# Sums of squares on VectorE alone, and another order of the paired units in a decoder layer

## The chip, the cores and the metric

The kernel runs on one core of a Trainium2 chip. The metric is the time of one execution in microseconds on the device (us), the median of several runs. The engines are called as in the profile: PE (TensorE, matmuls), PEld (its weight loads), DVE (VectorE), ACT (ScalarE), POOL (GpSimd) and SP (SyncE, whose queue issues the loads).

## The reference, cut to what matters

One decoder layer in fp32 on x of 1024 tokens by 1024 channels. The change touches the two feed-forward blocks and the gate columns of the projection in between, and the norms ahead of them:

```python
def rmsnorm(x, g):
    y = x * lax.rsqrt(jnp.mean(x * x, axis=-1, keepdims=True) + EPS)
    return y * g
def swiglu(x, w_gu, w_down):
    g, u = jnp.split(x @ w_gu, 2, axis=-1)
    return (jax.nn.silu(g) * u) @ w_down

x = x + 0.5 * swiglu(rmsnorm(x, ffn1_norm), ffn1_w_gu, ffn1_w_down)
h = rmsnorm(x, mix_norm);  z = h @ w_in
gates = jax.nn.sigmoid(z[..., COL_GATE:] + b_gate)
merged = gates_A * (y_a @ w_a) + gates_B * (y_b @ w_b) + gates_C * (y_c @ w_c)
x = x + merged @ w_out
x = x + 0.5 * swiglu(rmsnorm(x, ffn2_norm), ffn2_w_gu, ffn2_w_down)
```

## The kernel before

**Layout and precision.** The channels lie on the partitions, the tokens on the free axis, in two halves of 512. An x4 or w4 tile holds two rows of 128 channels by 512 tokens (128x1024). A matmul in fp32 is made of three in the type fp32r (`mm3`, L144 to L146): each operand is split into a high part, a cast on ACT (L132), and a low part, a subtraction on DVE (L133); the three products are high by high, high by low and low by high. `split_later` issues the cast and returns the subtraction as a function to be called later.

**Units.** `Seven` multiplies two by two blocks with seven products in place of eight. A unit f is one such block multiplication; its four blocks of weights are a11, a12, a22, a21, and four sums of them (s1 to s4) are made on DVE by `sums`. `weights` splits them in four parts: "a" (a11, a12), "s" (s2, s1), "t" (s3, s4), "l" (a22). The moving operands are the blocks of the normed x (b11, b12, b21, b22) and their sums t1 to t4, made and split by `OpNorm`. A product is four times three matmuls over the channels. Products go to banks of PSUM; partial sums are kept in SBUF rows: p1 is ACT's copy of a11 by b11, v1 is p1 plus s2 by t2. a12 by b21 is accumulated into the bank that p1 is copied from. `emit(f, i, half, ...)` finishes one quarter of the result: in `SwiGLU` a silu on ACT, additions and the gating multiplication on DVE, in `Gates` a sigmoid on ACT.

**Paired units.** Where the norm of the second half of the tokens is not ready, two units go together: `Seven.units`. It starts with the two products of each unit that need half 0 alone (s3, s4). Between their 16 pieces (counted by n) it places the sums over the channels of half 1 (`norm.tokens`, small matmuls of 128x1), the reciprocal root on DVE (`norm.root`) and the turn of the result into a row (`norm.turn`, PE transposes into a bank). Then follow a11, a12, s2, s1, and last a22 by t4. This happens at three places: units 1 and 2 of the first feed-forward block (the opening, from `SwiGLU.start`), units 0 and 1 of the gates, and units 0 and 1 of the second feed-forward block (ffn2). Behind each pair a single `unit` follows (3, 2 and 2). The functions in `asides` are called one by one at fixed places of `units`: the fetch of the next unit's weights and `ready`, which prepares its "a" part and its sums.

**Opening.** Unit 0 of the first block is multiplied in plain fp32 (`rows`: two matmuls a row of channels) while x arrives: `feed` squares a row on ACT and scales it with the gain; then sums of squares, root and turn follow for that half. The products are scaled by the norm afterwards: `leave` copies the banks, `keep` the scale, `finish` multiplies and does silu and gating.

**Sums of squares.** `square` issues a row's square and returns the addition into the half's accumulator (DVE). With `plain` no addition is made: the square is kept and the token sum, which is a matmul with a column of ones, takes one matmul more per 128 tokens for each such row.

**What sets the order.** In these three stretches the order on PE, DVE, ACT (and SP in the first two) is as the code is written, and each engine works through its instructions in that order.

Of the kernel before, what the change touches and what calls it, by code (L numbers as in the profile page):

```python
# [16 lines left out]
P = 128  # L17
# [25 lines left out]
class Kernel:  # L43
# [322 lines left out]

    def token_sums(self, accs, late=False, bank=None):


        n = accs[0].shape[-1] // P  # L370
        b = (bank or self.bank)()[:, :n]
        for t in range(n):
            for m, acc in enumerate(accs):
                i = self.nc.tensor.matmul(
                    b[:, t:t + 1], acc[:, t * P:(t + 1) * P], self.ones, start=m == 0, stop=m == len(accs) - 1)
                if late and t == 0 and m == 0:
                    self.after(i, self.last)
        return b
# [47 lines left out]
    def latent(self, h):  # L426
# [10 lines left out]
        def c_q(hf):  # L437
            acc, cols = None, slice(hf * 512, hf * 512 + 512)
            for j, d in enumerate(cq):
                b = self.bank()  # L440
                for k in range(DT):
                    self.mm3(b, w[j * DT + k], h[hf][k], k == 0, k == DT - 1)
                acc = self.norm_feed(acc, b, 512)
                self.split_gain(d[0][:, cols], d[1][:, cols], b, self.g_cq[:, j:j + 1])
            nc.vector.tensor_scalar(
                eps[:, hf * 4:hf * 4 + 4], self.token_sums([acc]), EPS / QR, EPS * EPS, op0=ALU.mult, op1=ALU.add)

# [223 lines left out]
    def mem_kv(self, p, filler):  # L671
# [4 lines left out]
        with tc.tile_pool(name="memkv", bufs=1) as q:  # L676
# [11 lines left out]
            fill(2)  # L688
            r = self.rms(self.token_sums([acc], late=True), ML // P, D)
            fill(2)  # L690
# [286 lines left out]
    def project(self, merged, norm, sink):  # L977

        nc, a = self.nc, self.a
        tasks = []  # L980
        for half in range(2):
            for c in range(DT):
                w = self.load(a["w_out"][c])
                b = self.bank()
                for k in range(DT):
                    self.mm3(b, w[k], merged[half][k], k == 0, k == DT - 1)
                x = norm.x(half, c)
                nc.vector.tensor_tensor(x, x, b, op=ALU.add)
                norm.feed(half, c, half == 1 and c == DT - 1)
# [17 lines left out]
    def run(self):  # L1007
# [12 lines left out]
        with tc.tile_pool(name="f1", bufs=1) as fp, self.banks("f1ps") as self.pm:  # L1020
# [15 lines left out]
            def sink(half, c):  # L1036
                add = norm.square(half, c, half == 1 and c >= DT - 2)
                keep(x1d, rows, half, c)
                return add
# [13 lines left out]
            with tc.manual_schedule(engines={E.PE, E.SP, E.DVE, E.Activation}):  # L1053
# [6 lines left out]
                     (6, 4): [do(gates.turned, 0), do(gates.sums, 1)]},  # L1060
                    late)
                gates.units(
                    (0, 1), {0: gates.w0[0], 1: {}}, ([(1, "t")], [(0, "a")]),
                    [lambda: None, do(gates.fetch, 2, [self.x4, gates.w4]), do(gates.ready, 2, [self.x4, gates.w4])])
                gates.unit(2, True)
# [4 lines left out]
        with tc.tile_pool(name="f2", bufs=1) as fp, self.banks("f2ps") as self.pm:  # L1070
# [9 lines left out]
            E = mybir.EngineType  # L1080
            with tc.manual_schedule(engines={E.PE, E.DVE, E.Activation}):
                ffn.units(
                    (0, 1), (), ([(0, "a"), (1, "a")], [(0, "s")]),
                    [lambda: None, lambda: ffn.fetch(2, [self.x4] * 2), lambda: ffn.ready(2)])
                ffn.spill(0, ffn.w4)
                ffn.unit(2, True)
# [22 lines left out]
class OpNorm:  # L1109
# [7 lines left out]
    def __init__(self, k, rows, gain, scaled=False):  # L1117
        self.k, self.x, self.t, self.gain, self.scaled = k, rows, rows, gain, scaled
        self.acc, self.r, self.s, self.op, self.rows, self.plain = {}, {}, {}, {}, {}, {}

    def feed(self, half, c, plain=False):
        self.square(half, c, plain)()

    def square(self, half, c, plain=False):

# [9 lines left out]

        if plain:
            self.plain.setdefault(half, []).append(sq)
            return lambda: None
        return add

    def tokens(self, half):
        k = self.k
        self.s[half] = k.token_sums(
            [self.acc.pop(half), *self.plain.pop(half, ())], late=k.last is not None)

# [73 lines left out]
class Seven:  # L1219
# [66 lines left out]
    def unit(self, f, after=False):  # L1286
# [3 lines left out]
        if not w:  # L1290
            self.sums(f)
            w |= self.weights(f, "a")
        w |= self.weights(f, "s")
        a, x, y = (k.single(), k.single(), k.bank()) if after else (k.bank(), k.single(), k.single())
# [23 lines left out]
    def ready(self, f, rooms=None):  # L1318

        self.made[f] = self.weights(f, "a")  # L1320
        self.sums(f, rooms)

    def units(self, fs, w=(), fill=((), ()), asides=()):
# [22 lines left out]
        for n, (u, (out, s, t), j) in enumerate(  # L1346
                (u, p, j) for u in fs for p in ((y[u], "s3", "t3"), (x[u], "s4", "b22")) for j in range(4)):
            self.product(out, w[u], s, t, js=(j,))
            if n == 1 and not known:
                norm.tokens(1)  # L1350
# [3 lines left out]
                for p in fill[1]:  # L1354
                    more(*p)
            if n == 4 and not known:
                norm.turn(1)
# [115 lines left out]
class SwiGLU(Seven):  # L1473
# [41 lines left out]
    def start(self, load_x, load_g):  # L1515
# [7 lines left out]

        def feed(half, c, plain=False):
            add = norm.square(half, c, plain)
            x, g = norm.x(half, c), norm.gain()[:, c:c + 1]
            if half == 0:
                v.tensor_scalar(x, x, g, None, op0=ALU.mult)
                add()
            else:  # L1530
# [39 lines left out]
        with k.tc.manual_schedule(engines={E.PE, E.DVE, E.Activation, E.SP}):  # L1570
# [29 lines left out]
            b22()  # L1600
            for c in (4, 5):
                feed(1, c, True)
            norm.high(1)
            norm.put("t3", 0, t3)
            leave(0)
            norm.low(1)
            for c in (6, 7):
                feed(1, c, True)
# [10 lines left out]
            leave(1)  # L1619
            self.units(  # L1620
                (1, 2), w, (),
                [lambda: keep(1), lambda: self.fetch(3, [k.x4] * 2), lambda: self.ready(3)])
            finish()
# [268 lines left out]
```

## Time and profile before

| | |
|---|---|
| runs | 2229.87, 2232.82, 2233.83 us; median 2232.82 |
| profiled execution | 2229.82 us, span 2228.1 us, mean granted PE clock 0.995 |
| busy: PE, DVE, ACT, POOL | 2199.7, 1542.7, 894.5, 259.3 us |
| paired units start: opening, gates, ffn2 | 47.3, about 670, about 1585 us |
| the unit behind the pair starts its second-last products | 102.40, 723.69, 1641.65 us |

Rows of the profile name engine, line, operation, tiles as out<-in, sizes and count. Times in a timeline are from the start of the span. A busy PE is one with a matmul under way; its granted clock is a share of the full clock. An fp32 matmul leaves two records, one in fp32r leaves one.

### The profile page before, as it was taken

The page shows a single profiled execution, that of the slowest core. Times are in us where ns is not written, and L with a number is a line of the kernel's source. Part 1 is how long each engine was busy: PE and PEld are TensorE (multiplying, and loading weights), DVE is VectorE, ACT ScalarE, POOL GpSimd, SP SyncE. Part 2 cuts the span into 40 slices and gives each one's busy share as a digit, 9 for nine tenths or more (in the row PEclk, how much of TensorE's full clock was granted, in tenths as well). Part 3 has the DMA queues.
Part 4 walks back from the last instruction along what each step waited for, and adds up shares of the span by engine and source line. Part 5 has one row for each costly group of instructions (what it writes and reads, how often), then busy time and mean ns, then how long its engine had stood idle before and what let it go on. Part 6 is the DMA issues. An engine that isn't in the chain of part 4 may idle for free.

```text
span 2228.1 us, 27721 instructions
## 1 busy us (share of the span) xinstructions
PE 2199.7 (99%) x10376; PEld 1834.7 (82%) x10376; DVE 1542.7 (69%) x2397; ACT 894.5 (40%) x1498; POOL 259.3 (12%) x252
## 2 busy tenths in 40 slices
PE   9899999999999999999999999999989999999999
PEld 5688888888887888888888889988878888888887
DVE  6866666679888655457575769885876666657784
ACT  5422222243455433344244559843432222224432
POOL 0121212100000000013000131140012121210000
PEclk9999999999999999999999999999999999999999
DMA  4233332285332333225161550084033333328543
GB/s 143 79 125 99 110 103 95 88 330 191 121 116 95 115 116 128 92 79 181 39 213 49 201 196 29 30 318 174 29 99 114 99 114 100 114 93 302 181 128 104
DMA packets 113062, 285.92 MB, mean 128 GB/s; under 512 B 13344, under 2 KB 21664, under 8 KB 112800
## 3 DMA queue, kind: packets, MB, share of 16 engines
q1 hardware_dynamic: 112928, 284.16, 37.1%
q8 instruction: 81, 1.33, 0.2%
q14 instruction: 53, 0.43, 0.1%
HBM read 201.80 MB, written 82.31 MB: 128 GB/s over the span
## 4 chain that ended last, share of the span: by engine, by line
PE 92%; DVE 5%; ACT 1%; issue 1%; DMA 0%; DVEq 0%; ACTq 0%
PE one L146 13%; PE bank L144 13%; PE one L144 13%; PE bank L146 13%; PE bank L145 13%; PE one L145 13%; PE mm L144 3%; PE mm L145 3%; PE mm L146 3%; PE bank L881 1%; PE bank L419 1%; PE bank L896 1%; DVE wlo L133 1%; PE bank L897 1%; PE one L1539 1%
## 5 line engine op out<-in xcount | busy, mean ns | idle before, releaser
L132 ACT CAST whi<-x 128x1024 fp32r<-128x1024 f32 (+1 forms) x189 | 178.8, 951 | 454.2 <-PE one L145 198.0
L1284 DVE TENSOR_TENSOR t<-t,one 128x512 f32<-128x512 f32 x178 | 122.2, 686 | 242.0 <-PE one L146 242.0
L144 PE MATMUL bank<-h,whi 128*128 128x512 f32 x644 | 250.8, 390 | 0.0
L145 PE MATMUL bank<-h,whi 128*128 128x512 f32 x644 | 250.7, 389 | 0.0
L146 PE MATMUL bank<-h,wlo 128*128 128x512 f32 x644 | 250.5, 389 | 0.0
L133 DVE TENSOR_TENSOR wlo<-x,whi 128x1024 fp32r<-128x1024 f32 (+1 forms) x189 | 226.7, 1204 | 33.5 <-ACT whi L132 33.5
L144 PE MATMUL one<-h,whi 128*128 128x512 f32 x476 | 186.1, 391 | 0.0
L146 PE MATMUL one<-h,wlo 128*128 128x512 f32 x476 | 185.3, 389 | 0.0
L145 PE MATMUL one<-h,whi 128*128 128x512 f32 x476 | 185.2, 389 | 0.0
L146 PE MATMUL one<-w,wlo 128*128 128x512 f32 x392 | 154.4, 394 | 5.6 <-DVE wlo L133 5.6
L144 PE MATMUL one<-w,whi 128*128 128x512 f32 x392 | 154.5, 394 | 5.5 <-ACT whi L132 5.5
L145 PE MATMUL one<-w,whi 128*128 128x512 f32 x392 | 154.1, 393 | 0.0
L127 ACT CAST whi<-w 128x1024 fp32r<-128x1024 f32 (+1 forms) x108 | 95.1, 899 | 143.7 <-PE one L145 55.2
L128 DVE TENSOR_TENSOR wlo<-w,whi 128x1024 fp32r<-128x1024 f32 (+1 forms) x108 | 110.1, 1033 | 60.6 <-ACT whi L127 60.5
L146 PEld LDWEIGHTS bank<-h,wlo 128*128 128x128 f32 x644 | 120.9, 188 | 25.2
L145 PEld LDWEIGHTS bank<-h,whi 128*128 128x128 f32 x644 | 120.9, 188 | 24.8
L144 PEld LDWEIGHTS bank<-h,whi 128*128 128x128 f32 x644 | 120.9, 188 | 24.8
L145 PE MATMUL bank<-wlo,whi 128*128 128x512 f32 x352 | 136.9, 389 | 0.0
L144 PE MATMUL bank<-whi 128*128 128x512 f32 x352 | 136.9, 389 | 0.0
L146 PE MATMUL bank<-whi,wlo 128*128 128x512 f32 x352 | 136.9, 389 | 0.0
L1636 POOL TENSOR_TENSOR raw<-raw 128x512 f32<-128x512 f32 x39 | 64.1, 1645 | 593.4 <-DVE raw L1494 593.4
L128 DVE TENSOR_TENSOR wlo<-h,whi 128x512 fp32r<-128x512 f32 x130 | 88.1, 713 | 26.5 <-ACT whi L127 26.5
(385 smaller groups left out, 5070.4 us busy)
## 6 DMA issues: line engine op xcount, KB each, us to landing
x<-in_ffn_w_gu_dram SPq DMA_DIRECT2D x78, 512.0 KB, 5.1
w<-tdt SPq DMA_DIRECT2D x40, 512.0 KB, 4.3
tdb<-raw SPq DMA_DIRECT2D x64, 256.0 KB, 2.1
h<-in_ffn_w_down_dram SPq DMA_DIRECT2D x64, 256.0 KB, 6.0
w<-tdb SPq DMA_DIRECT2D x30, 512.0 KB, 4.6
tdt<-w SPq DMA_DIRECT2D x48, 256.0 KB, 2.0
gate<-raw SPq DMA_DIRECT2D x23, 512.0 KB, 2.6
tdt<-raw SPq DMA_DIRECT2D x40, 256.0 KB, 3.1
```

The costliest lines, as they stand in the source:

```text
L127: self.nc.scalar.copy(hi, src)
L128: return (eng or self.nc.vector).tensor_tensor(lo, src, hi.bitcast(F32), op=ALU.subtract)
L132: self.nc.scalar.copy(hi, src)
L133: return lambda: self.nc.vector.tensor_tensor(lo, src, hi.bitcast(F32), op=ALU.subtract)
L144: mmul(out, s[0], m[0], start=first, stop=False, **kw)
L145: mmul(out, s[0], m[1], start=False, stop=False, **kw)
L146: self.last = mmul(out, s[1], m[0], start=False, stop=last, **kw)
L419: nc.tensor.transpose(b[:m, k * P:(k + 1) * P], s, self.ident)
L881: nc.tensor.transpose(b[:, at:at + P], prs[t][:, kk * P:(kk + 1) * P], self.ident)
L896: nc.tensor.matmul(o, w, pt[0], start=n == 0, stop=False)
L1284: return self.nc.vector.tensor_tensor(out, x, y, op=ALU.add)
L1636: sub = lambda d, x, y: nc.gpsimd.tensor_tensor(d, x, y, op=ALU.subtract)
```

## The change

Five edits:

- `plain` is gone: every square is added on DVE, and a token sum is four matmuls. There are 36 fewer small matmuls, and two more additions in half 0 of the opening, four in half 1, two in the gates and one in ffn2.
- In `units` the token sums stand behind piece 3 (were behind 1), the turn behind 6 (was 4). The cast and split of unit f's "s" weights goes ahead of the other unit's copy p1. At the end, the split of a unit's a22 and half of t4, the sum p1 and that unit's `emit` stand together, unit by unit; before, both units' splits came ahead of both sums.
- `ready` is now a generator in three steps. The cast of the next unit's "a" weights is issued ahead of the pair's first silu or sigmoid; its split, the sums, and the cast and split of "s" go ahead of the last additions, the gating, and in the opening `finish`. Before, "s" was cast and split in the next `unit`.
- The opening: sums and turn of half 0 stand behind rows 0 to 3 and row 4; additions go behind splits; in half 1 all of the norm stands behind row 5, and the turn behind row 7.
- In ffn2 other parts of the weights stand around the root (`fill`).

The diff, cut:

```diff
@@ token_sums @@
-        for t in range(n):
-            for m, acc in enumerate(accs):
-                i = self.nc.tensor.matmul(
-                    b[:, t:t + 1], acc[:, t * P:(t + 1) * P], self.ones, start=m == 0, stop=m == len(accs) - 1)
+        for t in range(n):
+            i = self.nc.tensor.matmul(
+                b[:, t:t + 1], acc[:, t * P:(t + 1) * P], self.ones, start=True, stop=True)
@@ gates and ffn2, the calls @@
+                third = gates.ready(2, [self.x4, gates.w4])
                 gates.units(
                     (0, 1), {0: gates.w0[0], 1: {}}, ([(1, "t")], [(0, "a")]),
-                    [lambda: None, do(gates.fetch, 2, [self.x4, gates.w4]), do(gates.ready, 2, [self.x4, gates.w4])])
+                    [lambda: None, do(gates.fetch, 2, [self.x4, gates.w4]), do(next, third), do(next, third)])
...
                 ffn.units(
-                    (0, 1), (), ([(0, "a"), (1, "a")], [(0, "s")]),
-                    [lambda: None, lambda: ffn.fetch(2, [self.x4] * 2), lambda: ffn.ready(2)])
+                    (0, 1), (), ([(0, "a")], [(1, "a")]),
+                    [lambda: None, lambda: ffn.fetch(2, [self.x4] * 2), lambda: next(third), lambda: next(third)])
@@ Seven.ready @@
-        self.made[f] = self.weights(f, "a")
+        self.made[f], low = self.weights_later(f, "a")
+        yield
+        low()
         self.sums(f, rooms)
+        self.made[f] |= self.weights(f, "s")
+        yield
@@ Seven.units @@
-            if n == 1 and not known:
+            if n == 3 and not known:
                 norm.tokens(1)
...
-            if n == 4 and not known:
+            if n == 6 and not known:
                 norm.turn(1)
...
             nc.scalar.copy(p1[u], a[u])
-        more(f, "s")
+            if u == f:
+                more(f, "s")
...
             d, low[u] = self.weights_later(u, "l")
             w[u] = {**w[u], **d}
+        aside()
         for u in fs:
             self.emit(u, 0, 1, None, a[u])
...
             low[u]()
             t4[p]()
-        for u in fs:
             self.mark = self.add(p1[u], p1[u], z[u])
             self.emit(u, 1, 0, p1[u], y[u])
@@ SwiGLU.start @@
-                feed(0, c, c >= 6)
+                feed(0, c)
             rows(0, range(4))
             norm.sums(0)
-            rows(0, (4, 5))
+            rows(0, (4,))
             norm.turn(0)
-            rows(0, (6, 7))
+            rows(0, (5, 6, 7))
...
-            rows(1, range(5))
-            norm.tokens(1)
+            rows(1, range(6))
+            norm.sums(1)
+            rows(1, (6, 7))
+            norm.turn(1)
             self.sums(2)
-            norm.root(1)
-            rows(1, (5, 6))
-            norm.turn(1)
-            rows(1, (7,))
             w[2] = self.weights(2, "t")
             leave(1)
```

**Half 1 of the opening on PE.** The rows named L1539 before and L1546 now are the plain matmuls of unit 0 (x_140 to x_146 are two rows of channels of half 1 each); 128x1 are token sums, 128x128 the turn, L144 the first piece of the pair. Before:

```order
L1539 MATMUL one<-x_144,w_122 128x512
L1539 MATMUL one<-x_144,w_123 128x512
L374 MATMUL bank<-ones,t 128x1 x20
L1539 MATMUL one<-x_144,w_122 128x512
L1539 MATMUL one<-x_144,w_123 128x512
L1539 MATMUL one<-x_146,w_122 128x512
L1539 MATMUL one<-x_146,w_123 128x512
L386 MATMUL bank<-ident,rs_y 128x128 x4
L1539 MATMUL one<-x_146,w_122 128x512
L1539 MATMUL one<-x_146,w_123 128x512
L144 MATMUL one<-h_268,whi 128x512
```

And now:

```order
L1546 MATMUL one<-x_144,w_122 128x512
L1546 MATMUL one<-x_144,w_123 128x512
L1546 MATMUL one<-x_144,w_122 128x512
L1546 MATMUL one<-x_144,w_123 128x512
L373 MATMUL bank<-ones,t 128x1 x4
L1546 MATMUL one<-x_146,w_122 128x512
L1546 MATMUL one<-x_146,w_123 128x512
L1546 MATMUL one<-x_146,w_122 128x512
L1546 MATMUL one<-x_146,w_123 128x512
L385 MATMUL bank<-ident,rs_y 128x128 x4
L144 MATMUL one<-h_262,whi 128x512
```

The sums moved behind one more row and are four instead of 20; the turn moved behind the last row.

**The end of the pair on DVE, in the opening.** L133 are splits: `wlo` of 128x512 a unit's a22, x4 of 128x1024 half of t4, `wlo` of 128x1024 the next unit's weights. L1284 (now L1281) are additions. Before:

```order
L133 TENSOR_TENSOR wlo_529<-w4_135,whi_528 128x512
L133 TENSOR_TENSOR x4_580<-x4_144,x4_579 128x1024
L133 TENSOR_TENSOR wlo_532<-w4_149,whi_531 128x512
L133 TENSOR_TENSOR x4_598<-x4_146,x4_597 128x1024
L1284 TENSOR_TENSOR t_470<-t_470,bank_538 128x512
L1284 TENSOR_TENSOR raw_534<-t_470,one_362 128x512
L1284 TENSOR_TENSOR t_472<-t_472,bank_551 128x512
L1284 TENSOR_TENSOR raw_536<-t_472,bank_364 128x512
L133 TENSOR_TENSOR wlo_633<-x4_486,whi_632 128x1024
```

And now:

```order
L133 TENSOR_TENSOR wlo_511<-w4_135,whi_510 128x512
L133 TENSOR_TENSOR x4_565<-x4_144,x4_564 128x1024
L1281 TENSOR_TENSOR t_452<-t_452,bank_523 128x512
L1281 TENSOR_TENSOR raw_519<-t_452,one_344 128x512
L133 TENSOR_TENSOR wlo_514<-w4_149,whi_513 128x512
L133 TENSOR_TENSOR x4_583<-x4_146,x4_582 128x1024
L1281 TENSOR_TENSOR t_458<-t_458,bank_536 128x512
L1281 TENSOR_TENSOR raw_521<-t_458,bank_346 128x512
L133 TENSOR_TENSOR wlo_517<-x4_468,whi_516 128x1024
```

The first unit's two additions moved ahead of the second unit's splits.

**The end of the pair and the start of unit 3 on ACT, in the opening.** L132 are casts (x4_564 and x4_582 now are t4; `whi` from x4_468, x4_618 and x4_619 are unit 3's "a", "s" and "t" weights), L1498 (now L1501) the pair's silus, L1565 (now L1572) those of `finish`, and the copy is p1 of unit 3. Before:

```order
L1498 ACTIVATE raw_534<-one_442 128x512
L1498 ACTIVATE raw_536<-one_455 128x512
L132 CAST x4_579<-x4_144 128x1024
L132 CAST x4_597<-x4_146 128x1024
L132 CAST whi_632<-x4_486 128x1024
L1498 ACTIVATE t_470<-t_470 128x512
L1498 ACTIVATE t_472<-t_472 128x512
L1565 ACTIVATE t_272<-t_272 128x512
L1565 ACTIVATE t_358<-t_358 128x512
L132 CAST whi_677<-x4_636 128x1024
L1297 COPY t_696<-one_681 128x512
```

And now:

```order
L132 CAST whi_516<-x4_468 128x1024
L1501 ACTIVATE raw_519<-one_424 128x512
L1501 ACTIVATE raw_521<-one_437 128x512
L132 CAST x4_564<-x4_144 128x1024
L132 CAST x4_582<-x4_146 128x1024
L132 CAST whi_624<-x4_618 128x1024
L1501 ACTIVATE t_452<-t_452 128x512
L1501 ACTIVATE t_458<-t_458 128x512
L1572 ACTIVATE t_268<-t_268 128x512
L1572 ACTIVATE t_340<-t_340 128x512
L1295 COPY t_678<-one_663 128x512
```

Unit 3's first cast moved ahead of the pair's first silus, its second from behind `finish` to ahead of the last four silus; the copy stays behind them.

More of the change, by code (lines that the diff above doesn't have):

```diff
@@ L365, in norm_feed, with token_sums @@
         return acc
-    def token_sums(self, accs, late=False, bank=None):
-        n = accs[0].shape[-1] // P
+    def token_sums(self, acc, late=False, bank=None):
+        n = acc.shape[-1] // P
         b = (bank or self.bank)()[:, :n]
         for t in range(n):
-            for m, acc in enumerate(accs):
-                i = self.nc.tensor.matmul(
-                    b[:, t:t + 1], acc[:, t * P:(t + 1) * P], self.ones, start=m == 0, stop=m == len(accs) - 1)
-                if late and t == 0 and m == 0:
-                    self.after(i, self.last)
+            i = self.nc.tensor.matmul(
+                b[:, t:t + 1], acc[:, t * P:(t + 1) * P], self.ones, start=True, stop=True)
+            if late and t == 0:
+                self.after(i, self.last)
         return b
@@ L445, in c_q @@
             nc.vector.tensor_scalar(
-                eps[:, hf * 4:hf * 4 + 4], self.token_sums([acc]), EPS / QR, EPS * EPS, op0=ALU.mult, op1=ALU.add)
+                eps[:, hf * 4:hf * 4 + 4], self.token_sums(acc), EPS / QR, EPS * EPS, op0=ALU.mult, op1=ALU.add)
         n, width = a["w_ckv"].shape[-1], KVR
@@ L688, in mem_kv @@
             fill(2)
-            r = self.rms(self.token_sums([acc], late=True), ML // P, D)
+            r = self.rms(self.token_sums(acc, late=True), ML // P, D)
             fill(2)
@@ L988, in project @@
                 nc.vector.tensor_tensor(x, x, b, op=ALU.add)
-                norm.feed(half, c, half == 1 and c == DT - 1)
+                norm.feed(half, c)
                 sink(half, c)
@@ L1036, in sink @@
             def sink(half, c):
-                add = norm.square(half, c, half == 1 and c >= DT - 2)
+                add = norm.square(half, c)
                 keep(x1d, rows, half, c)
@@ L1081, in run @@
             with tc.manual_schedule(engines={E.PE, E.DVE, E.Activation}):
+                third = ffn.ready(2)
                 ffn.units(
-                    (0, 1), (), ([(0, "a"), (1, "a")], [(0, "s")]),
-                    [lambda: None, lambda: ffn.fetch(2, [self.x4] * 2), lambda: ffn.ready(2)])
+                    (0, 1), (), ([(0, "a")], [(1, "a")]),
+                    [lambda: None, lambda: ffn.fetch(2, [self.x4] * 2), lambda: next(third), lambda: next(third)])
                 ffn.spill(0, ffn.w4)
@@ L1118, in __init__, with feed, square @@
         self.k, self.x, self.t, self.gain, self.scaled = k, rows, rows, gain, scaled
[L1119 to L1124, printed above, removed]
+        self.acc, self.r, self.s, self.op, self.rows = {}, {}, {}, {}, {}
+    def feed(self, half, c):
+        self.square(half, c)()
+    def square(self, half, c):
         k, acc = self.k, self.acc
@@ L1134, in add @@
                 acc[half] = sq
-        if plain:
-            self.plain.setdefault(half, []).append(sq)
-            return lambda: None
         return add
@@ L1142, in tokens @@
         k = self.k
-        self.s[half] = k.token_sums(
-            [self.acc.pop(half), *self.plain.pop(half, ())], late=k.last is not None)
+        self.s[half] = k.token_sums(self.acc.pop(half), late=k.last is not None)
     def root(self, half):
@@ L1292, in unit @@
             w |= self.weights(f, "a")
-        w |= self.weights(f, "s")
+        if "s2" not in w:
+            w |= self.weights(f, "s")
         a, x, y = (k.single(), k.single(), k.bank()) if after else (k.bank(), k.single(), k.single())
@@ L1522, in start, with feed @@
         scale, gate = [], []
-        def feed(half, c, plain=False):
-            add = norm.square(half, c, plain)
+        def feed(half, c):
+            add = norm.square(half, c)
             x, g = norm.x(half, c), norm.gain()[:, c:c + 1]
             if half == 0:
+                if c >= 6:
+                    add()
                 v.tensor_scalar(x, x, g, None, op0=ALU.mult)
-                add()
+                if c < 6:
+                    add()
             else:
@@ L1600, in start @@
             b22()
-            for c in (4, 5):
-                feed(1, c, True)
+            adds = [feed(1, c) for c in (4, 5)]
             norm.high(1)
-            norm.put("t3", 0, t3)
+            t3 = norm.put_later("t3", 0, t3)
+            for add in adds:
+                add()
+            t3()
             leave(0)
+            adds = [feed(1, c) for c in (6, 7)]
             norm.low(1)
-            for c in (6, 7):
-                feed(1, c, True)
+            for add in adds:
+                add()
             norm.apart(1)
             keep(0)
-            rows(1, range(5))
-            norm.tokens(1)
+            rows(1, range(6))
+            norm.sums(1)
+            rows(1, (6, 7))
+            norm.turn(1)
             self.sums(2)
-            norm.root(1)
-            rows(1, (5, 6))
-            norm.turn(1)
-            rows(1, (7,))
             w[2] = self.weights(2, "t")
             leave(1)
+            third = self.ready(3)
             self.units(
                 (1, 2), w, (),
-                [lambda: keep(1), lambda: self.fetch(3, [k.x4] * 2), lambda: self.ready(3)])
+                [lambda: keep(1), lambda: self.fetch(3, [k.x4] * 2), lambda: next(third), lambda: next(third)])
             finish()
```

## The prediction

> **What bounds the kernel now.** I read the page's first part, then the waits of PE, then the timelines of PE, VectorE (DVE) and ScalarE (ACT) in the three stretches that the change touches. Outside them every engine's order of instructions stays as it is.
>
> ```profile
> PE 2199.7 (99%) x10376; PEld 1834.7 (82%) x10376; DVE 1542.7 (69%) x2397; ACT 894.5 (40%) x1498; POOL 259.3 (12%) x252
> ...
> x<-in_ffn_w_gu_dram SPq DMA_DIRECT2D x78, 512.0 KB, 5.1
> ```
> ```profile
> PE one L144 <- DVE raw L1284: 5.7, 3, 2.0
> PE one L146 <- DVE wlo L133: 5.6, 3, 4.2
> ...
> PE one L144 <- ACT whi L132: 5.5, 2, 4.6
> ```
>
> PE is busy 2199.7 of 2228.1 us, so the program is bound by PE, and what can be won is PE work, PE waits, and PE work done at a low clock. In the waits (total, how many, longest) the three rows make 16.8 us in eight waits, all of them in the paired units of the three stages or just behind. Each is PE waiting for the end of a queue on DVE or ACT, so I follow those queues, and date each stage by the first product behind the pair whose start they set. Of PE in the opening:
>
> ```profile
> 13.41 2.76 PE L374 MATMUL bank<-ones,t 128*128 128x1 f32 x24
> ...
> 33.70 4.83 PE L374 MATMUL bank<-ones,t 128*128 128x1 f32 x40
> 38.39 6.75 PE L1539 MATMUL one<-x,w 128*128 128x512 f32 x8
> ...
> 45.42 1.88 PE L1539 MATMUL one<-x,w 128*128 128x512 f32 x4
> ...
> 82.85 0.47 PE L144 MATMUL one<-x,whi 128*128 128x512 f32 x1 [1.95 <-DVE raw L1284]
> ...
> 95.89 0.80 PE L144 MATMUL one<-w,whi 128*128 128x512 f32 x1 [4.61 <-ACT whi L132]
> ...
> 97.97 0.80 PE L146 MATMUL one<-w,wlo 128*128 128x512 f32 x1 [0.85 <-DVE wlo L133]
> ...
> 102.40 0.50 PE L144 MATMUL one<-h,whi 128*128 128x512 f32 x1
> ```
>
> The columns are start, time, engine, line, operation, count, and in brackets the idle time before it with what ended it. An fp32 matmul leaves two records, so x40 is the 20 token matmuls of half 1: 0.24 us each. 45.42 to 47.30 is the last pair of ffn1's opening rows, behind which the paired units start. The wait at 95.89 is for the second weights of unit 3, and 102.40 is that unit's a12. Stretches of the same and of the other stages (length, then busy time of PE, PEld, DVE, ACT, POOL, then granted clock, DMA share, GB/s):
>
> ```profile
> 33.80:38.50 4.70, 4.70 (x42) 4.70 (x40) 4.63 (x6) 1.53 (x2) 0.00 (x0) 0.92 0.01 2
> 38.50:45.40 6.90, 6.90 (x13) 2.99 (x13) 3.78 (x13) 1.04 (x1) 0.00 (x0) 0.56 0.00 0
> ```
> ```profile
> 709.00:713.40 4.40, 4.33 (x13) 3.40 (x14) 2.64 (x4) 2.38 (x3) 0.00 (x0) 0.64 0.02 4
> ```
> ```profile
> 1621.80:1627.40 5.60, 5.54 (x25) 4.63 (x26) 5.50 (x9) 0.00 (x0) 0.00 (x0) 1.00 0.27 94
> ```
> ```profile
> 1634.90:1638.90 4.00, 3.95 (x10) 3.12 (x11) 0.00 (x0) 0.00 (x0) 2.40 (x2) 0.57 0.46 174
> ```
>
> Behind the token sums the clock is 0.56 although PE counts as busy all through them: eight records take 6.75 us where four take 1.88 at full clock. It is low again in two of the later rows, behind waits. At a clock of 1.00, 25 records take 5.54, 0.222 each, so a product of 12 is some 2.7.
>
> **The opening's sums.** All squares are now added by DVE: four matmuls instead of 12 in half 0, four instead of 20 in half 1, at two and four more adds. DVE's queue there, and ahead of the pair's a22:
>
> ```profile
> 21.88 1.22 DVE L1161 TENSOR_TENSOR x<-x,bank 128x1024 f32<-128x1024 f32 x1 [1.08 <-PE bank L386]
> ...
> 34.53 2.42 DVE L133 TENSOR_TENSOR h<-x,h 128x1024 fp32r<-128x1024 f32 x2
> ...
> 39.52 0.15 DVE L172 TENSOR_SCALAR rms_v<-bank 128x4 f32<-128x4 f32 x1
> ...
> 41.29 0.16 DVE L165 SCALAR_TENSOR_TENSOR rs_y<-rs_b,rs_y 128x4 f32<-128x4 f32 x1
> ...
> 48.45 2.35 DVE L1161 TENSOR_TENSOR x<-x,bank 128x1024 f32<-128x1024 f32 x2 [5.86 <-ACT x L1550]
> ...
> 65.27 1.23 DVE L133 TENSOR_TENSOR wlo<-w,whi 128x1024 fp32r<-128x1024 f32 x1 [2.92 <-ACT whi L132]
> ...
> 87.72 0.68 DVE L1284 TENSOR_TENSOR t<-t,one 128x512 f32<-128x512 f32 x1
> ```
>
> Half 0: the tokens start about 1.6 later (two adds of 0.68 and their latency) and are eight matmuls of 0.23 shorter: about even, -0.25. The turn now stands behind one row instead of two, so the 1.08 of idle goes: DVE goes on 1.3 earlier. Half 1: four adds of 0.68 lengthen DVE's queue by 2.7, so its last split ends at 36.95 - 1.3 + 2.7 = 38.3; the last add lies some 2.3 (two splits) ahead, at 36.0, and PE waits for it. Four token matmuls end at 37.0, hidden under the splits. The root's small steps then go from 38.3 to 40.2 (1.9, as from 39.52 to the end of 41.29), and the four matmuls of rows 6 and 7 take 1.88 x 2 = 3.8 and end by 40.8: PE starts the pair some 6.4 earlier than 47.3. At the clock of 38.39 those rows would take 6.75 and end 3.0 later; that is this term's upper bound, and I take the full clock, since only one microsecond of small matmuls goes before.
>
> The wait of 5.86 at 48.45 is for ACT's keep(1). Now behind the root lie three more sums of unit 2 (2.0), their cast (1.05), two copies (1.2) and keep (0.6): 40.2 + 4.8 = 45.0, so DVE starts b11 3.45 earlier.
>
> **The opening's pair.** From 48.45 to 87.72 DVE takes 39.27. Its 2.92 of idle goes, since the cast of unit f's s weights now stands ahead of the copy that waits for PE. The split of unit 3's s weights (1.23) and the wait for its cast (1.05) come in ahead of the last gatings: 38.6, so 87.72 becomes 83.6. What follows is ACT's:
>
> ```profile
> 78.95 1.05 ACT L132 CAST whi<-x 128x1024 fp32r<-128x1024 f32 x1
> ...
> 93.67 1.23 ACT L1565 ACTIVATE t<-t 128x512 f32<-128x512 f32 x2 [4.01 <-DVE t L1564]
> ...
> 95.75 0.58 ACT L1297 COPY t<-one 128x512 f32<-128x512 f32 x1
> ```
>
> Now the cast of the s weights stands ahead of all silus, so s2 no longer waits for it. But unit 3's copy p1 still stands behind finish()'s two silus, and a12 accumulates into the bank that is copied. Those silus end 7.1 after 87.72 now (at 94.9); so then at 90.7, the copy at 91.25, and a12 goes from 102.40 to 91.25: -11.15. PE gets there at about 85.8: a22 waits for a sum that comes 3.45 and 2.92 earlier, and 1.8 more since the other unit's two splits (0.6 and 1.2) now stand behind it, 74.7 in place of 82.85; four products of 2.7 follow, and some 0.3 for the second half of t4. So this is a new wait of 5.4. How the clock takes it is the least known: the 13 records of 709.00 took 4.33 where 0.222 each makes 2.9, +1.4; ten at 1634.90 cost 1.7 more; twelve from 95.89 to 102.40 took 5.66 beside the wait of 0.85, +2.9. I take 1.7. Opening: -11.15 + 1.7 = -9.4; with bounds 0 and 2.9 on the clock, and 2.6 if the rows are slow, -11.2 to -5.6.
>
> [...]
>
> **The gates.**
>
> ```profile
> 709.07 0.47 PE L144 MATMUL one<-x,whi 128*128 128x512 f32 x1 [1.98 <-DVE raw L1284]
> ...
> 723.69 0.39 PE L144 MATMUL one<-h,whi 128*128 128x512 f32 x1
> ```
> ```profile
> 691.49 1.23 DVE L133 TENSOR_TENSOR wlo<-raw,whi 128x1024 fp32r<-128x1024 f32 x1 [0.83 <-ACT whi L132]
> ...
> 711.97 1.22 DVE L133 TENSOR_TENSOR wlo<-x,whi 128x1024 fp32r<-128x1024 f32 x1 [1.72 <-ACT whi L132]
> ```
> ```profile
> 718.95 1.03 ACT L132 CAST whi<-x 128x1024 fp32r<-128x1024 f32 x1
> 719.88 0.58 ACT L1297 COPY t<-one 128x512 f32<-128x512 f32 x1
> ```
>
> Sums: eight token matmuls fewer (1.9) against two adds (1.4) that now come first: taken as even, bounds -0.5 and +0.5. DVE loses idle of 0.83 and 1.72, and gains 0.5 (t4's casts behind the new cast of 1.03 on ACT, taken as half hidden) and 2.3 (s split and cast): its last adds come 0.3 later. The copy has no cast of 1.03 ahead of it, so it starts at 719.2 and a12 at 719.8: -3.9. Each sum now stands behind its own split, so a22 starts about 2.1 earlier, PE gets to a12 at 717.8 and waits 2.0. A low stretch of 1.4 there gives -2.5; without the copy's wait it is PE's 717.8, -5.9.
>
> **ffn2.**
>
> ```profile
> 1621.86 0.47 PE L144 MATMUL one<-x,whi 128*128 128x512 f32 x1 [1.78 <-DVE raw L1284]
> ...
> 1641.65 0.39 PE L144 MATMUL one<-w,whi 128*128 128x512 f32 x1
> ```
> ```profile
> 1605.42 2.36 DVE L133 TENSOR_TENSOR w<-x,w 128x1024 fp32r<-128x1024 f32 x2 [1.96 <-ACT w L132]
> ...
> 1626.74 0.68 DVE L1284 TENSOR_TENSOR t<-t,one 128x512 f32<-128x512 f32 x1
> ...
> 1631.37 1.33 DVE L1494 TENSOR_TENSOR raw<-raw,t 128x512 f32<-128x512 f32 x1
> ```
>
> Four token matmuls fewer against one add is even. DVE: idle of 1.96 goes, the s split of unit f comes back into the pair (+1.15), and +2.3 as above: the last adds begin 1.5 later, at 1628.2. a22 goes some 1.5 earlier (1.8 for the order of splits, the rest as in the gates), so s2 ends at 1631.2 and a12 at 1633.9. The sum v1 stands in DVE's queue behind the last gating (now at 1632.7), so at 1634.2, and ends at 1634.9; s1, which waits for it, goes from 1641.65 to 1634.9: -6.8. Bounds: a low stretch (+1.7) and no wait for v1 (-1.0): -7.8 to -5.1.
>
> The other edits cost nothing that I can see: 36 matmuls of 0.24 (8.6 us of PE) are in the terms above, no DMA is added, SP's and POOL's queues stay in order. Sum: -9.4 - 3.9 - 6.8 = -20.1, against the profiled execution's 2229.82: 2209.7. That execution was 3.0 below the median of the runs, 2232.82; so 2212.
>
> **The rivals.** (1) The new waits draw the clock down everywhere and the opening's rows are slow: +2.6 + 1.2 in the opening, +1.4 in the gates, +1.7 in ffn2 leave -13.2: 2220. For it speak the low rows; against, two of three waits of 2 us that left none. (2) ACT's copy doesn't hold a12, and PE's own arrival counts: 85.8 is 5.4 sooner and draws no clock (1.7), in the gates 2.0: -29.2, 2204. Against: ACT's queue has the copy behind the silus. (3) The change moves the waits only: DVE's queue, longer by nine adds and by splits ahead of the gatings, gives all back, 2230 to 2233. The idle that goes (2.92, 1.72, 1.96) and the earlier root speak against. (4) Slower: ACT works in order, and the cast of the next unit's first weights (78.95 now) goes ahead of the pair's silus, next to t4's casts. If its load lands late, silus, casts and PE wait for it.
>
> ```profile
> 28.11 0.43 SPq L1247 DMA_DIRECT2D x<-in_ffn_w_gu_dram  x1
> ```
>
> It outweighs the gain from 20.1 of lateness on; landing at 105, 26 after its present cast, gives +5.9: 2239. The issue stands 51 us ahead of that cast and such loads land in 5.1, against it.
>
> **How the numbers follow.** Chances: forecast 0.70, (1) 0.18, (2) 0.05, (3) 0.04, (4) 0.03. The forecast's own range is 2206 to 2218 (opening -11.2 to -5.6, gates -5.9 to -2.5, ffn2 -7.8 to -5.1, not all at one end); the range takes in (1) and the spread of the runs: 2204 to 2224. About 0.2%, 4.5 us, is what a measurement tells from no change: faster 0.92, the same 0.05, slower 0.03.
>
> **What would show it.** The pair of ffn1 starts near 41 in place of 47.3; a12 of unit 3 near 91 to 93 behind ACT's copy; the 4.61 and 4.2 waits for weights gone; a12 of the gates' unit 2 near 720 less the 9 won before, s1 of ffn2's at 1635 less 13. If rows 6 and 7 still take 6.75, or the wait for the copy is far from 5.4, a term is wrong; if a cast on ACT waits for a DMA, (4) is.

## The result, and the profile after

The changed kernel takes 2213.49 us (median of four runs, 2212.13 to 2214.99) against 2231.35 before: ratio 0.992, 95% interval 0.9903 to 0.9938. The forecast was 2212, in a range of 2204 to 2224. Its profiled execution took 2212.26 (span 2210.5), 17.6 less than the one before. The page's busy times and the first waits of PE (total, times, longest):

```profile
PE 2185.6 (99%) x10304; PEld 1820.8 (82%) x10304; DVE 1553.2 (70%) x2406; ACT 894.8 (40%) x1498; POOL 263.4 (12%) x252
```
```profile
PE one L144 <- ACT t L1295: 6.1, 2, 5.0
PE bank L373 <- DVE t L1133: 3.7, 2, 2.0
PE bank L385 <- DVE rs_y L165: 1.9, 2, 1.6
...
PE one L144 <- DVE t L1281: 1.2, 1, 1.2
```

The 16.8 us of waits for weights and for paired sums are gone but for 1.2, and in their place stand the waits that the prediction named: for ACT's copy (L1295) and for v1 (L1281). PE is busy 14.1 less; 36 matmuls at 0.24 are 8.6 of that, and the rest, 5.5, is about what the granted clock gives: its mean went from 0.995 to 0.998, by an estimate 0.003 of 2200, some 6.6. The rows of PE in the timeline that answer to those of before:

```profile
36.70 1.02 PE L373 MATMUL bank<-ones,t 128*128 128x1 f32 x8 [2.03 <-DVE t L1133]
37.59 3.68 PE L1546 MATMUL one<-x,w 128*128 128x512 f32 x8
41.11 0.60 PE L385 MATMUL bank<-ident,rs_y 128*128 128x128 f32 x4
...
74.98 0.47 PE L144 MATMUL one<-x,whi 128*128 128x512 f32 x1 [0.21 <-DVE raw L1281]
...
91.71 0.79 PE L144 MATMUL one<-h,whi 128*128 128x512 f32 x1 [5.01 <-ACT t L1295]
...
100.05 0.39 PE L144 MATMUL bank<-h,whi 128*128 128x512 f32 x1
```
```profile
710.92 0.50 PE L144 MATMUL one<-h,whi 128*128 128x512 f32 x1 [1.10 <-ACT t L1295]
...
1623.61 0.50 PE L144 MATMUL one<-w,whi 128*128 128x512 f32 x1 [1.17 <-DVE t L1281]
```

The sums end at 37.7 where 37.0 was forecast, a22 starts at 74.98 (74.7), a12 of unit 3 at 91.71 (91.25) behind a wait of 5.01 (5.4). The clock behind that wait, and the queue that ends it:

```profile
85.60:91.70 6.10, 1.10 (x5) 0.56 (x3) 5.99 (x9) 2.09 (x5) 0.00 (x0) 0.92 0.00 0
91.70:97.00 5.30, 5.29 (x13) 4.13 (x14) 5.24 (x6) 0.90 (x1) 3.86 (x3) 0.50 0.41 152
```
```profile
89.95 1.23 ACT L1572 ACTIVATE t<-t 128x512 f32<-128x512 f32 x2 [4.01 <-DVE t L1571]
91.09 0.57 ACT L1295 COPY t<-one 128x512 f32<-128x512 f32 x1
```

ACT's copy ends with a12's start, straight behind finish()'s two silus. Then 13 records take 5.29 at a clock of 0.50.

The gain by stage, from the starts of the same product in both profiled executions (a12 and s1, which the forecast dates, are the two products ahead of s3):

| stage | same product, before and after | gain in the stage | forecast |
|---|---|---|---|
| opening | unit 3's s3: 108.00, 100.05 | 7.95 | 9.4 |
| gates | unit 2's s3: 729.13, 716.49 | 4.7 | 3.9 |
| the stretch to ffn2 | the first piece of ffn2's pair: 1584.74, 1573.05 | -0.95 | 0 |
| ffn2 | unit 3's a12: 1657.97, 1640.38 | 5.9 | 6.8 |
| all | span 2228.1, 2210.5 | 17.6 | 20.1 |

The 0.95 is chance. No order differs in the stretch between, which took 856.56 here and 855.61 before, but 855.06 to 855.56 in three later profiled executions of the changed kernel. In this one DVE waits 2.18 for a load of the stored gates (1.14 and 0.65 before) and PE's wait for a root grows from 0.81 to 1.60.

```profile
1118.78 1.38 DVE L956 TENSOR_TENSOR t<-t,bank 128x512 f32<-128x512 f32 x2 [2.18 <-DMA t<-gate]
```
```profile
1124.43 0.43 PE L385 MATMUL bank<-ident,rs_y 128*128 128x128 f32 x2 [1.60 <-DVE rs_y L165]
```

### The profile page after: what moved, and what is told of

Its sections match the earlier page's. It is cut to its first block, busy times and chain, and to the rows that moved or that the text cites. A ratio compares the mean times of both kernels' runs of the same rounds, so it can differ in the third digit from the quotient of the medians.

```text
span 2210.5 us, 27597 instructions
## 1 busy us (share of the span) xinstructions
PE 2185.6 (99%) x10304; PEld 1820.8 (82%) x10304; DVE 1553.2 (70%) x2406; ACT 894.8 (40%) x1498; POOL 263.4 (12%) x252
## 4 chain that ended last, share of the span: by engine, by line
PE 89%; DVE 8%; ACT 1%; issue 1%; DMA 0%; SPq 0%; DVEq 0%; ACTq 0%
PE bank L144 13%; PE bank L145 13%; PE bank L146 13%; PE one L144 13%; PE one L145 13%; PE one L146 13%; PE mm L144 3%; PE mm L145 3%; PE mm L146 3%; PE bank L880 1%; DVE wlo L133 1%; PE bank L418 1%; PE bank L895 1%; PE bank L896 1%; DVE h L133 1%
## 5 line engine op out<-in xcount | busy, mean ns | idle before, releaser
L132 ACT CAST whi<-x 128x1024 fp32r<-128x1024 f32 (+1 forms) x189 | 179.5, 952 | 479.9 <-PE one L145 205.4
L1281 DVE TENSOR_TENSOR t<-t,one 128x512 f32<-128x512 f32 x178 | 122.2, 687 | 229.3 <-PE one L146 227.9
L144 PE MATMUL bank<-h,whi 128*128 128x512 f32 x644 | 250.8, 390 | 0.0
L133 DVE TENSOR_TENSOR wlo<-x,whi 128x1024 fp32r<-128x1024 f32 (+1 forms) x189 | 227.0, 1204 | 32.4 <-ACT whi L132 32.4
L144 PE MATMUL one<-h,whi 128*128 128x512 f32 x476 | 187.0, 393 | 6.1 <-ACT t L1295 6.1
L144 PE MATMUL one<-w,whi 128*128 128x512 f32 x392 | 152.9, 390 | 1.2 <-DVE t L1281 1.2
L144 PEld LDWEIGHTS bank<-h,whi 128*128 128x128 f32 x644 | 120.9, 188 | 25.0
L144 PE MATMUL bank<-whi 128*128 128x512 f32 x352 | 136.9, 389 | 0.0
L144 PEld LDWEIGHTS one<-h,whi 128*128 128x128 f32 x476 | 89.9, 189 | 26.1 <-ACT t L1295 7.1
```

The lines of the kernel that those rows point to most:

```text
L132: self.nc.scalar.copy(hi, src)
L133: return lambda: self.nc.vector.tensor_tensor(lo, src, hi.bitcast(F32), op=ALU.subtract)
L144: mmul(out, s[0], m[0], start=first, stop=False, **kw)
L1281: return self.nc.vector.tensor_tensor(out, x, y, op=ALU.add)
```

## The experiments

The theory of the prediction: the time is set where a queue on DVE or ACT ends last behind each pair, and PE's own work and earlier waits count only as far as they reach that point. The rival: what PE loses is what counts, each wait and each small matmul in full. Every group of kernels ran beside the changed kernel itself. The diffs show what matters, in places in fewer lines than the code has; three dots stand for lines left out.

> The changed kernel once more, as the measure for the kernels beside it: 2213.5 by its earlier median, within 1.5.

It took 2211.70, in the later groups 2212.37 and 2211.57; the comparisons below are with the one of the same group.

> The changed kernel as the measure for the kernels beside it: 2211.7 to 2213.5.

> The changed kernel as the measure for the kernels beside it: 2211.5 to 2213.5.

**The opening undone.**

```diff
-            rows(1, range(6))
-            norm.sums(1)
-            rows(1, (6, 7))
-            norm.turn(1)
+            rows(1, range(5))
+            norm.tokens(1)
             self.sums(2)
...
+            norm.root(1)
+            rows(1, (5, 6))
+            norm.turn(1)
+            rows(1, (7,))
             w[2] = self.weights(2, "t")
             leave(1)
```

(with the old order of half 0, of the additions, and the old squares in the opening).

> The opening alone goes back to its old order and its old sums (28 more small matmuls). If the queue that ends last sets the time: DVE starts b11 about 3.1 later (48.45 in place of 45.32), ACT's copy and a12 of unit 3 move with it, +3.1, though PE starts the pair 5.9 later. If PE's work counts: 28 matmuls of 0.24 and 3.1 of low clock on rows 6 and 7, +9.8. If what the opening's order won is hidden behind the wait for the copy: 0.

Measured 2216.69 against 2211.70, +5.0 (profiled spans 2215.0 and 2210.2, +4.8): more than the queues' 3.1, and about half of PE's sum. That sum was counted too high: the edit puts back 24 small matmuls (8 and 16), not 28, which makes it 8.9. PE is in fact busy 8.2 more (2195.1 against 2186.9), and 4.8 of it reach the end. DVE's rows in its timeline:

```profile
48.52 2.35 DVE L1163 TENSOR_TENSOR x<-x,bank 128x1024 f32<-128x1024 f32 x2 [5.81 <-ACT x L1559]
...
65.32 2.36 DVE L133 TENSOR_TENSOR w<-x,w 128x1024 fp32r<-128x1024 f32 x2 [1.49 <-ACT w L132]
```

b11 starts 3.5 later than in the same group's changed kernel (44.97), 0.4 more than expected. In the old order PE itself holds it: ACT's copies of the banks wait 6.35 for PE's last row (46.55), and the copy for which DVE waits 5.81 stands behind them. The row at 65.32 adds to it: DVE waits 1.49 for a cast that stands on ACT behind the second copy p1, and that copy waits for PE's a11. The changed kernel of the group waits 1.02 at the same place, so this adds 0.5, and another cast just ahead 0.2. a12 of unit 3 comes 4.3 later (96.77 for 92.46); the last 0.5 of the span fall in the stretch between the gates and ffn2, where no order differs. So PE's lateness does reach DVE's queue, through ACT's copies, and the theory as written had left the second of these links out.

**The sums alone.**

```diff
-            adds = [feed(1, c) for c in (4, 5)]
+            adds = [feed(1, c, True) for c in (4, 5)]
...
-            adds = [feed(1, c) for c in (6, 7)]
+            adds = [feed(1, c, True) for c in (6, 7)]
```

> In half 1 of the opening alone the last four squares go to the token sums on PE again (16 more small matmuls, four additions less on DVE); the order stays. If the queue that ends last sets the time: the sums need not wait 2.0 for the last addition but take 4.8 in place of 1.0, end about 1.8 later, and the root about 0.7 later than now: +0.7, up to +1.8. If PE's work counts: 16 matmuls of 0.24, +3.8.

Measured 2215.26 against 2212.37, +2.9 (spans 2213.5 and 2211.0, +2.5), above the one theory and below the other. b11 moves from 46.33 to 47.09, by the 0.7 expected; a22 from 77.07 to 78.80, by 1.0 more, the same link through PE's start (45.9 in place of 44.2): DVE's waits for casts behind the copies p1 make 1.9 there and 1.0 in the changed kernel. By unit 4 the two profiled executions are 2.0 apart. The rest lies within what runs of one kernel differ (2211.89 to 2214.86).

**The order of splits and sums undone.**

```diff
             low[u]()
             t4[p]()
+        for u in fs:
             self.mark = self.add(p1[u], p1[u], z[u])
```

> The splits of both units go ahead of both sums again, everything else stays. If the queue that ends last sets the time: a22 starts 1.8 later, but PE has a wait of 5.0 for the copy in the opening that takes it, 1.1 in the gates and 1.2 in the second feed-forward block: +0.7 and +0.4 at most there, +1 in all. If the waits for these sums are worth what the profile shows (5.7 before, 0.7 now): +5.0.

Measured 2217.93 against 2211.70 in the median, but the spans of the profiled executions, 2214.1 and 2210.2, differ by 3.9. By stages it is +0.4 in the opening, +1.4 in the gates, +0.9 in ffn2, and 1.2 in the stretch between where no order differs. The three waits are back:

```profile
77.89 0.47 PE L144 MATMUL one<-x,whi 128*128 128x512 f32 x1 [1.94 <-DVE raw L1281]
...
700.89 0.47 PE L144 MATMUL one<-x,whi 128*128 128x512 f32 x1 [1.98 <-DVE raw L1281]
...
1612.34 0.47 PE L144 MATMUL one<-x,whi 128*128 128x512 f32 x1 [1.96 <-DVE raw L1281]
```
```profile
700.80:704.90 4.10, 4.01 (x13) 3.21 (x14) 4.00 (x6) 1.45 (x2) 0.00 (x0) 0.69 0.00 0
1612.30:1616.40 4.10, 4.06 (x13) 3.22 (x14) 4.00 (x6) 0.00 (x0) 0.00 (x0) 0.68 0.39 131
77.80:80.70 2.90, 2.81 (x13) 2.36 (x13) 2.87 (x4) 0.00 (x0) 0.00 (x0) 1.00 0.45 162
```

In the opening the wait for the copy shrinks from 5.0 to 3.9 and takes most of it, as the theory has it. In the gates and ffn2 the clock behind the wait of 2.0 is also down, at 0.69 and 0.68, 13 records in 4.0 in place of 2.8: 1.2 each, which no later wait was long enough to take. Those 2.7 in the three stages are not the expected 1; the 5.0 of the rival is closer to the medians, and how much of the median's 6.2 is the edit stays open.

**The next unit's weights undone.**

```diff
-        self.made[f], low = self.weights_later(f, "a")
         yield
-        low()
+        self.made[f] = self.weights(f, "a")
         self.sums(f, rooms)
-        self.made[f] |= self.weights(f, "s")
         yield
```

> The next unit's first weights are cast and split where they were before: a behind t4, s in the unit itself. If the queue that ends last sets the time: a12 of unit 3 goes from 91.7 to 96.5 but without the low clock behind it, +2; the gates +4.8 and the second feed-forward block +6.3, less up to 2 that other edits took out of DVE's queue: +11 to +13. If this edit only traded waits: the weights' waits (4.61, 0.85, 0.93, 0.53, 4.23) come back and the new ones (5.0, 1.1, 1.2) go: +3.9.

Measured 2225.55 against 2211.70, +13.9 (spans 2222.8 and 2210.2, +12.6): three quarters of the change's whole gain. The spans give the theory's number, the medians 0.9 more than its range; PE is busy only 4.0 more (2190.9 against 2186.9). By stage +1.9, +5.3 and +5.8, where 2, 4.8 and 6.3 were expected. PE's rows:

```profile
90.24 0.80 PE L144 MATMUL one<-w,whi 128*128 128x512 f32 x1 [6.09 <-ACT whi L132]
...
713.34 0.79 PE L144 MATMUL one<-w,whi 128*128 128x512 f32 x1 [4.00 <-ACT whi L132]
...
1629.21 0.80 PE L146 MATMUL one<-w,wlo 128*128 128x512 f32 x1 [4.55 <-DVE wlo L133]
```

In the opening 6.09 comes in place of 5.01: there the edit has mostly traded one wait for another. In the other two stages waits of 4.00 and 4.55 stand against 1.09 and 1.15 in the changed kernel, so nearly all of the edit's gain is kept there.

The spans of the three kernels with one edit undone are 4.8, 3.9 and 12.6 longer, 21.3 together against the change's 17.6: the edits' gains overlap. The new places of the sums, the turn and the fill in the gates and ffn2 were not undone by themselves.

**finish() behind the copy.**

```diff
+        if then1:
+            then1()          # in unit(), behind the split of the t weights
         self.product(a, w, "a12", "b21", False)
...
-            finish()
             self.fetch(4, [k.x4] * 2)
-            self.spill(0, self.w4)
             self.hid[3] = self.w4()
-            self.unit(3, True)
+            self.unit(3, True, then1=lambda: (finish(), self.spill(0, self.w4)))
```

> finish() of the opening, and the stores behind it, go behind unit 3's copy p1 and its t weights; nothing else changes. If ACT's copy behind finish()'s silus is what a12 waits for, and the low clock follows from that wait: the 5.0 goes and the 2.6 of low clock with it, s1 then waits for v1 up to 0.9 behind the pair's gating: -6.5 to -7.5. If the low clock has another cause: -4.5. If DVE's queue takes the copy's place as the last (v1, the t split): -2 to -4.

Measured 2210.64 against 2212.37, -1.7; the ratios to before, 0.9908 (0.9891 to 0.9925) and 0.9921 (0.9908 to 0.9933), overlap, and the span of the profiled execution is not shorter (2211.4 against 2211.0): its a22 started 1.9 late, behind slower rows of unit 0 (6.46 for 5.38). Up to s3 the expectation holds: from a22 to s3 of unit 3 it takes 17.9 (78.95 to 96.84) where the changed kernel takes 24.2 (77.07 to 101.25), 6.3 less, and no matmuls stand 0.42 or 0.43 apart in a row, as those behind the wait of 5.02 do in the changed kernel. Then most of it is given back: from a22 to unit 4's a12 it takes 36.25 in place of 38.52, 2.3 less, which is the third of the expected cases. The next rows of PE:

```profile
96.84 0.39 PE L144 MATMUL bank<-h,whi 128*128 128x512 f32 x1
...
100.43 0.51 PE L144 MATMUL one<-h,whi 128*128 128x512 f32 x1 [0.70 <-DVE t L1281]
...
105.73 0.50 PE L144 MATMUL bank<-x,whi 128*128 128x512 f32 x1 [1.79 <-DVE w L1281]
```

Behind the wait of 1.79 the matmuls are slow again: they come to stand 0.42 or 0.43 apart, and 12 take 4.45 (105.73 to 110.18) in place of 2.7. What DVE and POOL do there, first with finish() moved, then in the changed kernel of the same group:

```profile
97.29 0.68 DVE L1252 TENSOR_TENSOR x<-x,x 128x512 f32<-128x512 f32 x1
97.89 0.68 DVE L1257 TENSOR_TENSOR x<-x 128x512 f32<-128x512 f32 x1
...
100.29 1.39 DVE L1255 TENSOR_TENSOR x<-x,x 128x512 f32<-128x512 f32 x1
101.72 1.68 DVE L1256 TENSOR_TENSOR x<-x,x 128x512 f32<-128x512 f32 x1
...
105.00 0.67 DVE L1281 TENSOR_TENSOR w<-t,bank 128x512 f32<-128x512 f32 x1
```
```profile
99.86 2.99 POOL L1650 TENSOR_TENSOR w<-raw 128x512 f32<-128x512 f32 x2 [72.83 <-DVE raw L1499]
...
104.50 1.72 POOL L1650 TENSOR_TENSOR raw<-raw 128x512 f32<-128x512 f32 x1
106.17 2.26 POOL L1650 TENSOR_TENSOR w<-raw,w 128x512 f32<-128x512 f32 x1
```
```profile
95.67 1.40 DVE L1252 TENSOR_TENSOR x<-x,x 128x512 f32<-128x512 f32 x1
96.99 1.76 DVE L1257 TENSOR_TENSOR x<-x 128x512 f32<-128x512 f32 x1
```
```profile
95.24 2.96 POOL L1645 TENSOR_TENSOR w<-raw 128x512 f32<-128x512 f32 x2 [67.78 <-DVE raw L1497]
```

The same two additions of DVE (97.29 and 97.89; 95.67 and 96.99) take 0.68 ahead of POOL's subtractions, and 1.40 and 1.76 beside them: the slow ones move with POOL. The addition that reads a bank (105.00) takes 0.67 while POOL runs (104.50). So when the wait for the copy is gone, PE waits for DVE's queue, which is longer by finish() and slower beside POOL.

**POOL's part taken away, as meant.**

```diff
             finish()
             self.fetch(4, [k.x4] * 2)
-            self.spill(0, self.w4)
             self.hid[3] = self.w4()
             self.unit(3, True)
+            self.spill(0, self.w4)
```

> finish() stays, but spill(0) of the opening (four subtractions on POOL and seven stores) goes behind unit 3. If POOL's subtractions are what stretches DVE's from 0.68 to 1.4 to 2.3 in unit 3: those durations fall to 0.68 and 1.22 there, PE's wait of 0.5 at the product behind s3 goes, the wait of 5.0 and the low clock stay: -0.5. If DVE is slowed by something else (the loads, the copies): durations stay and so does the time.

> finish() goes behind unit 3's t weights as in the kernel before, and spill(0) behind unit 3. If that kernel's gain of 6.3 up to s3 was given back because POOL's subtractions then ran beside the splits of unit 4 that PE waited for: the waits of 0.70 and 1.79 go and 5 to 6.5 of the gain stay, 2206 to 2207. If DVE's queue is late there on its own account (finish()'s six operations, 4.4): the waits stay, -1.5 as before, 2210 to 2211.

The first took 2213.45 against 2211.57, +1.9 and no gain (spans 2210.9 and 2209.7), the second, which has both moves, 2209.74, -1.8 (span 2206.5, -3.2). Neither tests POOL, whose order the code does not fix: its subtractions started at 93.76 in the first, where the changed kernel has them at 93.68, and at 96.34 in the second. DVE's operations there stayed slow, so how much of the giving back is POOL's and how much finish()'s own DVE time stays open. That time is five operations and 3.8 (1.28, 1.22 and 1.29 for two, one and two of them), not the six and 4.4 of the expectation. In the second kernel s3 comes 6.4 sooner (93.28 for 99.69) and in unit 4's last products 2.8 are left; the rows of PE that lose the rest:

```profile
102.13 0.50 PE L146 MATMUL bank<-h,wlo 128*128 128x512 f32 x1 [2.21 <-DVE wlo L133]
...
113.81 0.50 PE L144 MATMUL one<-w,whi 128*128 128x512 f32 x1 [0.96 <-DVE t L1281]
```

**The same in all three stages.** Two versions:

```diff
-        for then in [self.emit(u, 0, 0, p1[u], x[u], p1[u]) for u in fs]:
+        def first():      # additions and silus or sigmoids of (0, 0)
...
+        def second():     # gating and (1, 1)
...
-                gates.unit(2, True)
+                gates.unit(2, True, then0=lambda: (first(), second()))   # behind copy p1
...
+                first()
-                ffn.spill(0, ffn.w4)
-                ffn.unit(2, True)
+                ffn.unit(2, True, then1=second)                          # behind the t split
+                ffn.spill(0, ffn.w4)
```

(the first with the stores inside then1, as in the kernel with finish() moved).

> As the kernel with finish() behind the copy, and in the gates the pair's last additions and sigmoids go behind the next unit's copy p1, in the second feed-forward block the last gating and the stores go behind v1 and the t weights. If each wait counts in full: -1.1 and -1.2 beside that kernel's gain, -9 in all. If their places are taken by other waits (the t split behind the sigmoids' additions, the bank of a silu): the gain of that kernel alone, -7.

> The same, with the pair's end behind the next unit's first steps in the gates and in the second feed-forward block too, and spill(0) of that block behind unit 2. If waits for copy, v1 and POOL's share are all there is: the gates 1.0 and the second block 1.0 to 1.5 more than the kernel with finish() and spill(0) moved, 2204 to 2205. If the pair's gating makes the next splits late in its turn: no more than that kernel.

Measured 2210.81 against 2212.37, and 2209.02 against 2211.57: -1.6 and -2.5. The second is the lowest median of all, but its ratio to before, 0.9905 (0.9891 to 0.9918), overlaps with the changed kernel's 0.9917 (0.9904 to 0.9931): the difference is a tenth of a per cent and not shown. The span of its profiled execution is only 0.4 shorter (2209.3 against 2209.7). By stage that one wins 1.4 more in the gates, where the wait of 1.10 is gone, and loses 1.9 in ffn2, where 1.14 at s1 goes and 1.81 comes two products on, at DVE's next addition, with matmuls up to 0.43 apart behind it (12 in 4.10 in place of 2.7). The move in the opening and the gates without that in ffn2 was not tried.

## Why the prediction was right

- **The order of the queues carried it.** a12 behind the copy, the copy behind finish()'s silus, s1 behind v1: each new wait is in the trace at its place, 5.01, 1.10 and 1.17. Rival (2), a copy that holds nothing, fell with that row. The kernel with the weights' edit undone gives +12.6 in the span where the queues gave 11 to 13 and a trade of waits 3.9.
- **The opening was over-sized by 1.5.** a12 came 0.5 late, and from there to s3 it took 2.7 more than before (8.34 for 5.60), where 1.7 was taken for the low clock. Of it 2.4 lie in the 13 records of 5.29, at 0.222 each otherwise. The trace of before had shown 2.9 behind a wait of nearly the same length, and that nearest row was the better price here; in the three later profiled executions the 12 matmuls took 4.6 to 4.7, 1.9 to 2.0 more than 2.7.
- **The gates were under-sized by 0.8.** a12 came at 710.92, 4.8 sooner against the start of the stage, with a wait of 1.10 for the forecast 2.0, and without a low stretch. PE got there as forecast. The copy came sooner, since DVE's last additions, which were taken as 0.3 later, came 0.7 sooner (715.76 before, 707.12 now, with the stage's start 7.95 earlier).
- **ffn2 was over-sized by 0.9.** s1 came 6.35 sooner (1641.65, 1623.61), since DVE's last additions and v1 ended 0.3 to 0.4 later than forecast, and another 0.45 went in the products behind it. There the stores' subtractions on POOL fall on unit 2's additions, which take 1.77 for 0.68, and no term had POOL in it; that the 0.45 are POOL's is not shown.
- **The full clock on rows 6 and 7** was luck. It held in the profiled execution (3.68 for eight records) and in none of the three later ones of the same kernel (5.38 in each, at 0.67 in the first). The reason given, one microsecond of small matmuls, did not count PE's wait of 2.03 ahead of them, which is there in all four, so neither is shown to decide. It cost little: in the first of the three b11 started no later, at 44.97, but a cast behind PE's a11 held DVE for 1.02, and their spans are 2209.7 to 2211.0 against 2210.5. The bound of 2.6 was too wide and the chain through the copy p1 was missing. Rows of PE and DVE in that execution:

```profile
37.24 5.38 PE L1546 MATMUL one<-x,w 128*128 128x512 f32 x8
```
```profile
61.02 2.36 DVE L133 TENSOR_TENSOR w<-x,w 128x1024 fp32r<-128x1024 f32 x2 [1.02 <-ACT w L132]
```

- **Sums even in the gates and ffn2, loads not late:** no cast on ACT waits for a DMA in the three stages. Rival (4) had nothing behind it. Of rival (1) the slow rows came true in those three executions, at 1.0 on DVE in place of 2.6; behind the new waits in the gates and ffn2 (1.10 and 1.17) the clock was 1.00 in the profiled execution (710.9 to 714.0, 1623.6 to 1627.0).

The sum, 20.1 against 17.6, was right to an eighth, by errors of both signs (1.5, 0.8 and 0.9) and a chance delay of 0.95 between. The path was right; that the sizes came so close is in part luck.

## What to carry to other kernels

Price a change by the queue that ends last: follow the in-order engine from the edit to the first product that cannot start without it, and ask what stands ahead of that in the same queue; a wait of PE that vanishes is worth only what the next wait leaves of it. Put work that the next stage needs ahead of work that only finishes the last one, but count the finishing work again where it lands: here two thirds of the 6.3 won at one product were lost within the next five. And a wait of PE can also have a price in the clock behind it: here all thirteen waits of 3.87 to 6.09 had one, and of the twelve waits of 1.78 to 2.21 in the pairs and the units behind them six had one and six had none.

## What the runs showed of the hardware

- A wait of PE of about 2 us was followed by slow matmuls in some places and not in others, and its length did not decide. In the pairs and the units behind them, waits of 1.98 (before, 709.07, and with the order undone, 700.89), 1.96 (order undone, 1612.34), 1.84 and 1.81 (the first and the second version in all three stages, 104.83 and 1627.08) and 1.79 (finish() moved, 105.73) had matmuls up to 0.43 apart behind them, 12 in 3.98 to 4.45 us; the granted clock was 0.64, 0.69 and 0.68 at the first three. Behind waits of 1.78 and 1.95 (before, 1621.86 and 82.85), 1.94 (order undone, 77.89), 1.80 (the first version in all three stages, 1628.55), 2.20 (the second, 103.36) and 2.21 (both moves, 102.13) they stood 0.22 to 0.24 apart but for the first step, 12 in 2.80 to 2.86 where no other wait came in; the clock was 1.00 at the first three. At the same product of ffn2 it was thus 1.80 with at most 0.24 in one of the two last kernels and 1.81 with up to 0.43 in the other. Behind all thirteen waits of 3.87 to 6.09 the matmuls stood 0.42 or 0.43 apart, seven or more in a row; the clock was 0.50 to 0.59 at five of them (two before, one each in the changed kernel's first two profiled executions and with the opening undone). Behind all those of 0.93 to 1.17 they stood 0.22 to 0.24 apart but for the first step and where another wait came in; the clock was 1.00 at the changed kernel's two.
- DVE's additions and subtractions of two operands of 128x512 in SBUF took 0.68 each ahead of POOL's subtractions (finish() moved, 97.29 and 97.89); beside them they took 1.39 and 1.68 (the same kernel, 100.29 and 101.72), and 1.40 and 1.76 in the changed kernel (95.67 and 96.99). Additions that read a PSUM bank took 0.67 while POOL ran (finish() moved, 105.00; both moves, 102.00).
